# A diffusion layer on one core: key/value projection in groups of two, four and four chunks, and the modulation loads put last with three of their eight blocks kept whole

## The chip, the core and the metric

The kernel runs on one core of a Trainium2 chip. A core has a matrix engine (TensorE, PE in the views), three engines for elementwise work (VectorE or DVE, ScalarE or ACT, GpSimd or POOL), a queue engine that issues transfers (SyncE, SP) and sixteen DMA engines behind it. Each engine runs its own instructions in order and waits on semaphores for the others. The metric is the device time of one execution in microseconds; the median of several runs counts.

## What is computed

One layer of a diffusion backbone. Everything the change touches lies at its start: the modulation vectors, the modulated norm of the tokens, and the keys and values.

```python
def adaln(cvec, w_mod, b_mod):
    m = jax.nn.silu(cvec) @ w_mod + b_mod          # (1024) @ (1024, 6144)
    return jnp.split(m, 6, axis=-1)                # shift 1, scale 1, gate 1, shift 2, ...

def modulate(x, g, shift, scale):
    return rmsnorm(x, g) * (1 + scale) + shift

def keys_values(h, w_kv, k_gain):
    k, v = jnp.split(h @ w_kv, 2, axis=-1)         # (n, 1024) @ (1024, 256)
    k = rmsnorm(k.reshape(b, n, N_KV_HEADS, HEAD_DIM), k_gain)
    return k, v.reshape(b, n, N_KV_HEADS, HEAD_DIM)

def hybrid_layer(...):
    sh1, sc1, ... = adaln(c, w_mod, b_mod)         # for the 1024 latent tokens
    csh1, csc1, ... = adaln(c_ctx, w_mod, b_mod)   # for the 256 context tokens
    hl, hc = modulate(xl, g_mix, sh1, sc1), modulate(xc, g_mix, csh1, csc1)
    kc, vc = keys_values(hc, w_kv, k_gain)
    kl, vl = keys_values(hl, w_kv, k_gain)
    ...   # queries, attention, spatial gating, output projection, mixture of 16 experts
```

All is in float32, and the weights of the experts make up most of the bytes that are read.

## The kernel before

A product that has to be as good as float32 is made of three products of a rounded format, float32r: each operand is split into a rounded part `hi` (ScalarE casts, line 147) and the rest `lo` (a subtraction, line 148, on VectorE or GpSimd), and TensorE adds hi·hi, hi·lo and lo·hi. `split_to` does this for weights.

**Modulation.** Of the 6144 columns of `w_mod` the start needs 2048, shift and scale. They come as eight blocks of 512 rows by 512 columns (1 MB each, `mod_load`), two blocks to a group of 512 columns. `mod_rows` splits a block and multiplies it by `c4`, which holds the two conditioning vectors, hi and lo, as four columns: the vectors are the stationary side, the 512 weight columns stream past, 4 row slices times 2 products a block (lines 255 and 256), and the result is four rows of 512 numbers in `pr`. `mod_columns` copies these rows out (line 260) and turns them into columns with four small float32 products against `sel4` (line 262; each is two instructions in the trace). All land in `pm1`; `modc` adds the bias (line 296) and `G1` is the gain times one plus the scale (line 297).

**Tokens.** There are ten chunks of 128 tokens, 0 to 7 latent and 8 and 9 context. `x_load` loads one (0.5 MB), `x_prep` squares and sums it on ScalarE (line 165), takes the root on VectorE and GpSimd (lines 84 and 85) and scales the chunk on VectorE (line 168). `x_steps` is a generator that lets the first half of the next chunk run ahead of the second half of this one. `modulate` works on one slice j of 128 channels of one group of chunks: TensorE turns each chunk's slice (line 187), ScalarE multiplies by `G1` and adds the shift into `h` (line 191, two buffers), VectorE rounds (line 193), and VectorE or GpSimd subtracts (line 195; `LOW_P` names the slices whose subtraction goes to GpSimd).

**Keys and values.** `kv_group` takes one group of chunks, runs over the eight slices, and per slice and chunk issues three products of 256 columns (lines 219 to 221), with `modulate` two slices ahead and one or two steps of a `side` generator behind each slice. Groups are chunks 0 to 3, 4 to 7, and 8 and 9. During the first group the side work is `x_steps` of chunks 4 to 7; during the other two it is that of 8 and 9 and then `w_steps`, which splits eight quarter blocks of the next projection with GpSimd subtracting.

The order of all this is written out by hand, instruction by instruction (`manual_schedule`); no scheduler moves anything. SyncE's queue is: blocks 0 and 1, small vectors, blocks 2 to 7, chunks 0 to 3, the key/value weights, chunks 4 to 7, the next weights (2 MB), chunks 8 and 9. Behind the stage the projections of the gating and the queries start (lines 722 to 724).

Further down `g_unit` makes other columns of the modulation with float32 products that stay whole, four for each of eight groups (line 397):

```python
            for b_ in range(4):
                nc.tensor.matmul(gs["pm"][:, b_:b_ + 1], gs[cb - 1][:, b_ * P:(b_ + 1) * P], onec, start=True, stop=True)
```

Of the kernel before, what the change touches and what calls it, by code (L numbers as in the profile page):

```python
# [47 lines left out]
def layer(ctx: ExitStack, tc: tile.TileContext, a, out, dbg=None):  # L48
# [62 lines left out]
    def gm_tiles(dt):  # L111
        return [gms.tile([P, 2048], dt, name=f"gm{i}") for i in range(2)]
# [67 lines left out]
    LOW_P = ((2, 4, 6), (), ())  # L180

    def modulate(g, n, j):

        i = 1 if g == 2 else 0
        pt = psA.tile([P, 512], F32, name="tp", bufs=3)[:, :n * P]
        for t in range(n):
            nc.tensor.transpose(pt[:, t * P:(t + 1) * P], XS[g * 4 + t][:, j * P:(j + 1) * P], ident)
        h = xs.tile([P, 512], F32, name="h", bufs=2)[:, :n * P]
        pv, hv = (w.rearrange("p (t c) -> p t c", t=n) for w in (pt, h))
        parts = [(slice(0, 2), HA[0]), (slice(2, 4), HA[1])] if g == 0 else [(slice(0, n), HH1 if g == 1 else HHC[0])]  # L190
        nc.scalar.activation(h, pt, AF.Identity, scale=G1[:, j, i:i + 1], bias=B1[:, j, i:i + 1])
        for t, hi in parts:
            nc.vector.tensor_copy(hi[:, :, j, :], hv[:, t])
        for t, hi in parts:
            (nc.gpsimd if j in LOW_P[g] else nc.vector).tensor_tensor(HL[g][:, t, j, :], hv[:, t], hi[:, :, j, :].bitcast(F32),
                                                                      op=OP.subtract)

    def kv_group(g, side, steps):

        n = 2 if g == 2 else 4  # L200
        ps = [psA.tile([P, 512], F32, name="pj", bufs=4) for _ in range(n)]
        if g == 0:
            modulate(g, n, 0)
            modulate(g, n, 1)
            split_to(*wkv2, rkv[:, 2:4, :])
        for j in range(DJ):
            if j + 2 < DJ:
                modulate(g, n, j + 2)
            elif g < 2:

                if g == 1 and j + 2 == DJ:
                    gmc = [w.rearrange("p (t j c) -> p t j c", t=2, j=DJ) for w in gm_tiles(F32R)]
                    HHC.append(gmc[0])
                    HL.append(gmc[1])
                modulate(g + 1, 4 if g == 0 else 2, j + 2 - DJ)
            for t in range(n):
                hh = (HHC[0][:, t] if g == 2 else h_part(0, g * 4 + t))[:, j, :]
                hl = HL[g][:, t, j, :]
                nc.tensor.matmul(ps[t][:, :256], hh, wkv[j // 4][0][:, j % 4, :], start=(j == 0), stop=False)
                nc.tensor.matmul(ps[t][:, :256], hh, wkv[j // 4][1][:, j % 4, :], start=False, stop=False)  # L220
                nc.tensor.matmul(ps[t][:, :256], hl, wkv[j // 4][0][:, j % 4, :], start=False, stop=(j == DJ - 1))
            for _ in range(steps[j]):
                next(side, None)
        for t in range(n):
            kt = g * 4 + t
            nc.scalar.copy(kraw[:, kt], ps[t][:, :128].rearrange("p (g d) -> p g d", g=NKV))
            nc.scalar.copy(V[:, kt * NKV:(kt + 1) * NKV], ps[t][:, 128:256].rearrange("p (g d) -> p g d", g=NKV))
# [7 lines left out]
    wraw += [rawp.tile([P, 4, 512], F32, name="raw") for _ in range(2)]  # L235
    CB = (2, 3, 0, 1)

    def mod_load(n):
        nc.sync.dma_start(wraw[n], rows(a["w_mod"], n % 2 * 512, 512, CB[n // 2] * 512, 512))

    def mod_rows(n):
        jh = n % 2
        if jh == 0:
            XS["pr"] = psA.tile([P, 512], F32, name="pj", bufs=4)
        pr = XS["pr"]
        pair = w_pair()
        if n < 7:
            for h in range(2):
                split_to(*pair[h], wraw[n][:, h * 2:h * 2 + 2, :])
        for jj in range(4):  # L250
            j = jh * 4 + jj
            wh, wl = w_part(pair, jj)
            if n == 7:
                split_to(wh, wl, wraw[n][:, jj, :])
            nc.tensor.matmul(pr[:4, :], c4[:, j, :], wh, start=(j == 0), stop=False)
            nc.tensor.matmul(pr[:4, :], c4[:, j, :], wl, start=False, stop=(j == DJ - 1))

    def mod_columns(n, pr):
# [13 lines left out]
    pr = None  # L272
    for n in range(8):
        mod_rows(n)
        if n == 2:
            pv = psA.tile([P, 512], F32, name="tp", bufs=3)
            nc.tensor.transpose(pv[:, :NV], vecs, ident[:NV, :NV])
            nc.vector.tensor_copy(colv, pv[:, :NV])
            gmixc, gffnc, bmodc, bsc, gfc = (colv[:, i:j] for i, j in ((16, 24), (24, 32), (32, 80), (80, 88), (88, 96)))
        if n % 2 == 0 and n:  # L280
            mod_columns(n // 2 - 1, pr)
        pr = XS["pr"]
        if n == 3:
            rkv = wraw[2]
            for h in range(2):
                nc.sync.dma_start(rkv[:, h * 2:h * 2 + 2, :].rearrange("p a b -> p (a b)").rearrange(
                    "p (j c) -> p j c", j=4), rows(a["w_in"], h * 512, 512, 512, 256))
            for kt in range(4, 8):
                x_load(kt)
    wkv = w_pair()  # L290
    xst = x_steps(range(4))
    next(xst)
    mod_columns(3, pr)
    for _ in range(2):
        next(xst)
# [1385 lines left out]
```

## Time and profile before

| | |
|---|---|
| median of 3 runs | 1770.59 us (1770.58 to 1771.48) |
| the profiled execution | 1771.12 us, of which the span of its instructions is 1769.4 us |
| TensorE busy | 1704.0 us (96%) |
| VectorE busy | 1558.7 us (88%) |
| ScalarE busy | 1269.7 us (72%) |
| GpSimd busy | 510.0 us (29%) |
| mean granted TensorE clock | 0.987 of 2.4 GHz |
| first key/value product | 38.21 us |
| first product behind the stage | 80.67 us |

Times in the views count from the first instruction. A row of a timeline gives the start, the length, the engine, the source line, what is written from what, how many were merged, and in brackets how long the engine had been idle and what released it. Products overlap in the array, so the length of one (0.40 us at 512 columns) is more than the distance to the next (0.23 us). A row of stretches gives, for each engine, busy time and number of instructions, then the granted TensorE clock (1.00 is 2.4 GHz, 0.50 is 1.2 GHz), the DMA engines' share and GB/s.

### The profile page before, as it was taken

How to read it: one execution, taken by the hardware profiler on the slowest of the kernel's cores; microseconds unless marked ns; L12 is line 12 of the kernel's file. 1: busy time of each engine (PE TensorE's matmuls, PEld its weight loads, DVE VectorE, ACT ScalarE, POOL GpSimd, SP SyncE). 2: the span in 40 equal slices, each digit the busy share in tenths (PEclk: the TensorE clock that was granted, in tenths of full speed). 3: DMA queues.
4: the chain of work that ended last, by engine and by line, in shares of the span. 5: the costliest groups of instructions: out<-in, count | busy, mean ns of one | idle time of the engine just before them, and what ended most of it. 6: DMA issues, size and time to landing. Idle time of an engine off the chain costs nothing.

```text
span 1769.4 us, 24698 instructions
## 1 busy us (share of the span) xinstructions
PE 1704.0 (96%) x8586; PEld 1406.0 (79%) x8586; DVE 1558.7 (88%) x2329; ACT 1269.7 (72%) x1705; POOL 510.0 (29%) x358
## 2 busy tenths in 40 slices
PE   7999989999999979999999999999999999999997
PEld 3888878888888758777778888888888888888885
DVE  7778777888748999999999999999999999999997
ACT  6632367888853357777778887887878878878886
POOL 1433466788831203232330110101101101101013
PEclk9999999999999979999999999999999999999999
DMA  9357200000035678999999999999999999999994
GB/s 356 99 158 235 84 1 1 25 25 1 13 136 211 214 288 307 363 361 362 341 373 383 392 382 383 386 385 374 389 383 377 387 384 377 389 386 385 374 329 182
DMA packets 204973, 485.71 MB, mean 275 GB/s; under 512 B 10448, under 2 KB 12848, under 8 KB 204848
## 3 DMA queue, kind: packets, MB, share of 16 engines
q1 hardware_dynamic: 200096, 466.83, 71.3%
q0 software_dynamic: 4752, 17.30, 3.8%
q8 instruction: 67, 1.10, 0.3%
q14 instruction: 58, 0.48, 0.1%
HBM read 463.13 MB, written 20.97 MB: 274 GB/s over the span
## 4 chain that ended last, share of the span: by engine, by line
PE 83%; DVE 11%; issue 3%; ACT 2%; POOL 1%; DMA 0%; POOLq 0%; SPq 0%; DVEq 0%; ACTq 0%
PE p L1598 25%; PE p L1601 12%; PE py L1588 6%; PE py L1587 6%; PE py L1589 6%; PE po L801 4%; DVE wlo L148 2%; PE pj L722 2%; PE pj L724 2%; PE pj L723 2%; PE tp L1387 2%; PE st L779 2%; PE st L778 2%; PE ap L661 1%; PE pj L1023 1%
## 5 line engine op out<-in xcount | busy, mean ns | idle before, releaser
L148 DVE TENSOR_TENSOR wlo<-raw,whi 128x1024 fp32r<-128x1024 f32 (+1 forms) x544 | 646.4, 1231 | 43.2 <-ACT whi L147 39.4
L147 ACT CAST whi<-raw 128x1024 fp32r<-128x1024 f32 (+1 forms) x578 | 585.6, 1029 | 114.2 <-PE p L1601 67.8
L789 POOL TENSOR_TENSOR pl<-pf,ph 128x512 fp32r<-128x512 f32 x160 | 207.8, 1322 | 52.6 <-ACT ph L787 32.9
L1598 PE MATMUL p<-whi,xb 128*128 128x512 f32 x512 | 205.0, 400 | 0.0
L1598 PE MATMUL p<-whi,xa 128*128 128x512 f32 x512 | 204.7, 400 | 0.0
L1598 PE MATMUL p<-wlo,xa 128*128 128x512 f32 x512 | 200.0, 391 | 0.3 <-DVE wlo L148 0.2
L1598 PE MATMUL p<-wlo,xb 128*128 128x512 f32 x512 | 199.8, 390 | 0.0
L1588 PE MATMUL py<-wlo,thl 128*128 128x512 f32 x504 | 198.4, 394 | 0.0
L1587 PE MATMUL py<-whi,thl 128*128 128x512 f32 x504 | 197.6, 392 | 0.0
L1589 PE MATMUL py<-whi,thl 128*128 128x512 f32 x504 | 196.3, 389 | 0.0
L1601 PE MATMUL p<-whi,xb 128*128 128x512 f32 x512 | 158.1, 390 | 0.4 <-DVE xb L1550 0.4
L1601 PE MATMUL p<-whi,xa 128*128 128x512 f32 x512 | 158.0, 390 | 0.0
L148 DVE TENSOR_TENSOR wlo<-H,whi 128x1024 fp32r<-128x1024 f32 x106 | 131.6, 1266 | 9.6 <-ACT whi L147 8.6
L148 DVE TENSOR_TENSOR wlo<-gm,whi 128x1024 fp32r<-128x1024 f32 (+1 forms) x111 | 133.1, 1220 | 6.5 <-ACT whi L147 6.0
L147 ACT CAST whi<-H 128x1024 fp32r<-128x1024 f32 x110 | 115.9, 1054 | 24.2 <-PE p L1601 17.9
L147 ACT CAST whi<-gm 128x1024 fp32r<-128x1024 f32 (+1 forms) x111 | 114.7, 1045 | 15.7 <-PE py L1589 8.3
L1405 POOL DMA_INDIRECT acc<-ye,idx x15 | 38.1, 2539 | 292.1 <-DVE ye L1402 292.1
L787 ACT CAST ph<-pf 128x512 fp32r<-128x512 f32 x160 | 99.3, 621 | 28.4 <-PE po L801 25.8
L1601 PEld LDWEIGHTS p<-whi,xb 128*128 128x128 f32 x512 | 96.0, 188 | 21.7 <-DVE xb L1550 0.8
L1601 PEld LDWEIGHTS p<-whi,xa 128*128 128x128 f32 x512 | 96.1, 188 | 20.9
L1598 PEld LDWEIGHTS p<-wlo,xa 128*128 128x128 f32 x512 | 96.3, 188 | 19.5 <-DVE wlo L148 1.1
L1587 PEld LDWEIGHTS py<-whi,thl 128*128 128x128 f32 x504 | 94.6, 188 | 21.6
(379 smaller groups left out, 3691.4 us busy)
## 6 DMA issues: line engine op xcount, KB each, us to landing
raw<-in_w_dram SPq DMA_DIRECT2D x271, 1024.0 KB, 8.3
H<-in_w_dram SPq DMA_DIRECT2D x55, 1024.0 KB, 8.0
gm<-in_w_dram SPq DMA_DIRECT2D x54, 1024.0 KB, 8.5
raw<-in_w_mod_dram SPq DMA_DIRECT2D x64, 256.0 KB, 3.2
raw<-in_w_mod_dram SPq DMA_DIRECT2D x4, 1024.0 KB, 7.5
raw<-in_w_in_dram SPq DMA_DIRECT2D x16, 256.0 KB, 4.0
raw<-in_w_out_dram SPq DMA_DIRECT2D x4, 1024.0 KB, 5.1
xr<-in_x_dram SPq DMA_DIRECT2D x8, 512.0 KB, 6.2
```

The source lines that it names most:

```text
L147: nc.scalar.copy(hi, src)
L148: (eng or nc.vector).tensor_tensor(lo, src, hi.bitcast(F32), op=OP.subtract)
L722: nc.tensor.matmul(p, hh[:, j, :], hi, start=(j == 0), stop=False)
L787: nc.scalar.copy(ph, pf)
L789: nc.gpsimd.tensor_tensor(pl, pf, ph.bitcast(F32), op=OP.subtract)
L801: nc.tensor.matmul(U["po", u][:, sl], st[:, blk], mv[:, sl], start=(k == 0 and o == 0 and n == 0), stop=(k == NK - 1 and n == 2), skip_gro ...
L1405: nc.gpsimd.indirect_dma_start(out=acc, out_offset=bass.IndirectOffsetOnAxis(ap=idx[:, e:e + 1], axis=0), in_=G["ye"], in_offset=None, com ...
L1587: nc.tensor.matmul(PY[e][cb], th, hi[:, sl], start=fst, stop=False)
L1588: nc.tensor.matmul(PY[e][cb], th, lo[:, sl], start=False, stop=False)
L1589: nc.tensor.matmul(PY[e][cb], tl, hi[:, sl], start=False, stop=lst)
L1598: nc.tensor.matmul(p, xh[:, j, :], w[:, jj, :], start=(j == 0 and w is pr[0]), stop=False)
L1601: nc.tensor.matmul(p, xl[:, j, :], pr[0][:, jj, :], start=False, stop=(j == DJ - 1))
```

## The change

Three things are changed at the start of the kernel; from the gating projection on, each engine's instructions stand in the order of before.

1. **Groups.** `GROUPS` makes the first key/value group of chunks 0 and 1, the second of 2 to 5 and the third of 6 to 9, so that the context chunks are in the last group, beside two latent ones. In that group ScalarE's shift is two instructions of 256 columns a slice, since latent and context have different vectors. GpSimd also subtracts slices 2, 4 and 6 of the second group. The rounded context slices live in a ring of four slots in one buffer.
2. **Queue.** The loads are: blocks 0 to 3, chunk 0, block 4, chunk 1, block 5, the key/value weights, blocks 6 and 7 as four quarters each, chunks 2 to 7. The key/value weights are split, and the first three slices of chunks 0 and 1 turned, before blocks 6 and 7 are used.
3. **Whole blocks.** Blocks 3, 5 and 7 (`FULL`) are not split. `mod_full` multiplies them as float32: 16 products a block, in which the 128 by 128 weights are the stationary side and two columns of `csil` (the two conditioning vectors) stream past; the sums add to `pm1` directly.

```diff
+    GROUPS = ((0,), (1, 2), (3, 4))
+    LOW_P = ((2, 4, 6), (2, 4, 6), ())
...
+    def turn(g, j):
+
+        pt = XS["pt", g, j] = psA.tile([P, 512], F32, name="tp", bufs=3)
+        for i, kt in enumerate(2 * q + t for q in GROUPS[g] for t in range(2)):
+            nc.tensor.transpose(pt[:, i * P:(i + 1) * P], XS[kt][:, j * P:(j + 1) * P], ident)
+
+    def modulate(g, j):
+
+        if ("pt", g, j) not in XS:
+            turn(g, j)
+        n = len(GROUPS[g]) * 2 * P
+        pt = XS.pop(("pt", g, j))
+        h = xs.tile([P, 512], F32, name="h", bufs=2)
+        for i, sl in ((0, slice(0, 2 * P)), (1, slice(2 * P, n))) if g == 2 else ((0, slice(0, n)),):
+            nc.scalar.activation(h[:, sl], pt[:, sl], AF.Identity, scale=G1[:, j, i:i + 1], bias=B1[:, j, i:i + 1])
+        hv = h.rearrange("p (q t c) -> p q t c", q=2, t=2)
+        for k, q in enumerate(GROUPS[g]):
+            nc.vector.tensor_copy(h_pair(q, j)[0], hv[:, k])
+        for k, q in enumerate(GROUPS[g]):
+            hi, lo = h_pair(q, j)
+            (nc.gpsimd if j in LOW_P[g] else nc.vector).tensor_tensor(lo, hv[:, k], hi.bitcast(F32), op=OP.subtract)
...
-            for _ in range(steps[j]):
+            for _ in range(2 if g == 0 and j < 2 else 1):
                 next(side, None)
...
+    FULL = (3, 5, 7)
+
     def mod_load(n):
-        nc.sync.dma_start(wraw[n], rows(a["w_mod"], n % 2 * 512, 512, CB[n // 2] * 512, 512))
+        src = rows(a["w_mod"], n % 2 * 512, 512, CB[n // 2] * 512, 512)
+        if n < 6:
+            nc.sync.dma_start(wraw[n], src)
+        else:
+            for jj in range(4):
+                nc.sync.dma_start(wraw[n][:, jj, :], src[:, jj, :])
...
+    def mod_full(n, jjs):
+        for jj in jjs:
+            for b in range(4):
+                nc.tensor.matmul(pm1[:, CB[n // 2] * 4 + b, :], wraw[n][:, jj, b * P:(b + 1) * P], csil[:, 4 + jj, :],
+                                 start=False, stop=False, skip_group_check=True)
...
-    for n in range(2, 8):
-        mod_load(n)
-    for kt in range(4):
+    mod_load(2)
+    mod_load(3)
+    x_load(0)
+    mod_load(4)
+    x_load(1)
+    mod_load(5)
+    mod_rows(0)
+    mod_rows(1)
+    pv = psA.tile([P, 512], F32, name="tp", bufs=3)
+    nc.tensor.transpose(pv[:, :NV], vecs, ident[:NV, :NV])
+    nc.vector.tensor_copy(colv, pv[:, :NV])
...
+    mod_rows(2)
...
+    mod_load(6)
+    mod_load(7)
+    for kt in range(2, 8):
         x_load(kt)
...
+    mod_columns(0)
+    mod_full(3, range(4))
+    mod_columns(1)
+    xst = x_steps((0, 1))
+    next(xst)
+    mod_rows(4)
+    next(xst)
+    mod_full(5, range(4))
+    mod_columns(2)
+    for _ in xst:
+        pass
     wkv = w_pair()
...
+    for h in range(2):
+        split_to(*wkv[h], rkv[:, h * 2:h * 2 + 2, :])
+    for j in range(3):
+        turn(0, j)
+    mod_rows(6)
+    mod_full(7, range(4))
+    mod_columns(3)
...
-    kv_group(0, x_steps(range(4, 8)), (1, 1, 2, 2, 2, 1, 1, 1))
-    ws = chain(x_steps((8, 9)), w_steps())
-    kv_group(1, ws, (1,) * 8)
-    kv_group(2, ws, (1,) * 8)
+    ws = chain(x_steps(range(2, 6)), x_steps(range(6, 10)), w_steps())
+    for g in range(3):
+        kv_group(g, ws)
```

TensorE, from the end of block 2 to the end of block 4 (`pj` are the sums of rows, `pk` is `pm1`, `HL1` and `HH1` hold raw blocks 3 and 5). Before, block 3 follows as eight wide products and the columns of blocks 0 and 1 were made in the middle of block 2:

```order
L256 MATMUL pj_191<-wlo_195,c4_80 4x512
L277 MATMUL tp_208<-ident_68,vecs_119 128x96
L262 MATMUL pk_130<-sel4_71,h_211 128x2 x4
L255 MATMUL pj_191<-whi_217,c4_80 4x512
L256 MATMUL pj_191<-wlo_218,c4_80 4x512
```

And now:

```order
L276 MATMUL pj_188<-wlo_192,c4_80 4x512
L289 MATMUL pk_130<-sel4_71,h_223 128x2 x4
L281 MATMUL pk_130<-csil_79,HL1_133 128x2 x16
L289 MATMUL pk_130<-sel4_71,h_245 128x2 x4
L275 MATMUL pj_261<-whi_262,c4_80 4x512
L276 MATMUL pj_261<-wlo_263,c4_80 4x512
```

Between the wide products of blocks 2 and 4 there now stand 24 narrow ones in a row, of two columns each, where eight wide ones and four narrow ones stood.

ScalarE, around the start of the key/value stage (`jk,r` are the squares, `gm` holds chunks 4 to 7). Before, the squares of the first four chunks stand ahead of the first shift:

```order
L147 CAST whi<-raw 128x512 x4
L165 ACTIVATE jk,r<-x 128x1024 x4
L147 CAST whi<-HL_133 128x1024
L191 ACTIVATE h<-tp,modc,G_83 128x512 x2
L147 CAST whi<-HL_133 128x1024
L191 ACTIVATE h<-tp,modc,G_83 128x512
```

And now:

```order
L147 CAST whi<-raw 128x512 x4
L207 ACTIVATE h<-tp,modc,G_83 128x256 x3
L165 ACTIVATE jk,r<-x 128x1024 x2
L207 ACTIVATE h<-tp,modc,G_83 128x256
L165 ACTIVATE jk,r<-gm_128 128x1024
```

The squares of chunks 2 to 5 now stand behind the first three shifts, so behind `G1`, and among the shifts of the first group.

SyncE's queue. Before:

```order
L239 DMA HL1_133<-in_w_mod_dram 128x4x512 x2
L239 DMA HH1_134<-in_w_mod_dram 128x4x512 x2
L239 DMA raw_135<-in_w_mod_dram 128x4x512
L239 DMA raw_136<-in_w_mod_dram 128x4x512
L157 DMA x_150<-in_x_dram 128x1024
```

And now:

```order
L157 DMA x_146<-in_x_dram 128x1024
L256 DMA HH1_134<-in_w_mod_dram 128x4x512
L157 DMA x_149<-in_x_dram 128x1024
L256 DMA HH1_134<-in_w_mod_dram 128x4x512
L311 DMA HL1_133<-in_w_in_dram 128x4x256 x2
L259 DMA raw_135<-in_w_mod_dram 128x512 x4
L259 DMA raw_136<-in_w_mod_dram 128x512 x4
```

Two chunks and the key/value weights, 2 MB together, have moved ahead of the last two blocks.

## Rows read from the trace of the kernel before

**Rows 1.** The page of the whole run: the chain that ended last, shares by engine.

```profile
PE 83%; DVE 11%; issue 3%; ACT 2%; POOL 1%; DMA 0%; POOLq 0%; SPq 0%; DVEq 0%; ACTq 0%
```

**Rows 2.** Stretches: busy us of each engine, granted clock, DMA share, GB/s.

```profile
80.60:130.00 49.40, 49.40 (x256) 42.05 (x256) 32.29 (x53) 18.78 (x39) 15.87 (x13) 1.00 0.59 190
```

**Rows 3.** Timeline of ScalarE: start, length, line, operation, then idle time and its releaser.

```profile
23.52 2.00 ACT L147 CAST whi<-raw 128x1024 fp32r<-128x1024 f32 x2 [0.71 <-DMA raw<-in_w_mod_dram]
...
26.23 2.18 ACT L147 CAST whi<-raw 128x512 fp32r<-128x512 f32 x4 [0.71 <-DMA raw<-in_w_mod_dram]
```

**Rows 4.** Timeline of VectorE and TensorE around the third modulation block.

```profile
13.68 2.36 DVE L148 TENSOR_TENSOR wlo<-HL,whi 128x1024 fp32r<-128x1024 f32 x2 [0.71 <-ACT whi L147]
...
14.53 0.40 PE L255 MATMUL pj<-whi,c 128*4 128x512 f32 x1
...
17.13 0.26 DVE L278 COPY colv<-tp 128x96 f32<-128x96 f32 x1 [1.10 <-PE tp L277]
```

**Rows 5.** Timeline of TensorE at 2.4 GHz, and one line's group over the run.

```profile
28.49 1.05 PE L262 MATMUL pk<-sel,h 4*128 4x2 f32 x8
...
29.47 0.39 PE L255 MATMUL pj<-whi,c 128*4 128x512 f32 x1
...
29.70 0.40 PE L256 MATMUL pj<-wlo,c 128*4 128x512 f32 x1
...
102.48 0.95 PE L397 MATMUL pk<-onec,g 128*128 128x1 f32 x8
...
L397 PE MATMUL pk<-onec,g x64: 164/250/250, 102.5 to 200.3; 128*128 128x1 f32 x64
```

**Rows 6.** Timeline of TensorE later in the run, at 1.2 GHz, two wide products.

```profile
240.62 0.63 PE L778 MATMUL st<-HL,K 128*128 128x512 f32 x1
...
241.04 0.63 PE L779 MATMUL st<-HL 128*128 128x512 f32 x1
```

**Rows 7.** TensorE later in the run: sixteen narrow products, and the stretch they fill.

```profile
269.18 2.28 PE L764 MATMUL tp<-wr,modl 128*128 128x16 f32 x16
...
270.00:271.00 1.00, 1.00 (x9) 1.00 (x8) 0.00 (x0) 0.04 (x1) 0.00 (x0) 0.71 0.00 0
```

**Rows 8.** Timeline from the end of the modulation to the first key/value product.

```profile
33.34 0.19 DVE L296 TENSOR_TENSOR modc<-pk,colv 128x32 f32<-128x32 f32 x1 [0.42 <-PE pk L262]
...
33.57 0.17 DVE L297 SCALAR_TENSOR_TENSOR G<-modc,colv 128x16 f32<-128x16 f32 x1
...
35.57 0.75 DVE L168 TENSOR_SCALAR x<-x,r 128x1024 f32<-128x1024 f32 x1 [0.44 <-POOL r L85]
...
36.38 2.18 PE L187 MATMUL tp<-ident,x 128*128 128x128 f32 x9 [0.72 <-DVE x L168]
...
38.21 0.56 PE L219 MATMUL pj<-whi,H 128*128 128x256 f32 x1
```

**Rows 9.** Stretches around the start of the key/value stage: the granted clock.

```profile
35.00:41.00 6.00, 5.10 (x23) 4.81 (x24) 5.31 (x13) 4.07 (x7) 0.53 (x1) 0.50 1.03 397
...
42.00:48.00 6.00, 6.00 (x54) 6.00 (x53) 4.70 (x14) 5.08 (x10) 4.32 (x7) 1.00 0.34 123
```

**Rows 10.** Stretches of the second and the third key/value group as they run before.

```profile
54.77:69.30 14.53, 14.53 (x125) 14.38 (x123) 11.18 (x19) 10.63 (x23) 6.48 (x6) 1.00 0.04 12
...
69.30:80.67 11.37, 8.32 (x60) 7.21 (x59) 9.94 (x15) 6.38 (x17) 6.33 (x5) 1.00 0.04 11
```

**Rows 11.** Groups by form, 0 to 82 us: ScalarE's shifts and squares.

```profile
L191 ACT ACTIVATE h<-tp,modc,G 128x256 f32<-128x256 f32 x8 | 4.5, 566 | 4.8 <-DVE gm L195 3.3 <-DVE HL L195 0.7 <-PE tp L187 0.4
...
L165 ACT ACTIVATE jk<-x 128x1024 bf16<-128x1024 f32 x6 | 6.4, 1070 | 1.2 <-issue 1.1
```

**Rows 12.** VectorE's rounding alone and beside GpSimd, and GpSimd's subtractions, same stretch.

```profile
70.51 0.28 DVE L193 CAST gm<-h 128x256 fp32r<-128x256 f32 x1
...
72.28 1.08 DVE L193 CAST gm<-h 128x256 fp32r<-128x256 f32 x1 [0.22 <-ACT h L191]
...
L148 POOL TENSOR_TENSOR wlo<-raw,whi 128x512 fp32r<-128x512 f32 x8 | 11.4, 1438 | 6.5 <-ACT whi L147 6.1
```

More of the change, by code (lines that the diff above doesn't have):

```diff
@@ L178, in x_steps @@
             yield
[L180 to L196, printed above, removed]
@@ L198, in kv_group, with h_pair @@
-    def kv_group(g, side, steps):
-        n = 2 if g == 2 else 4
-        ps = [psA.tile([P, 512], F32, name="pj", bufs=4) for _ in range(n)]
+    GROUPS = ((0,), (1, 2), (3, 4))
+    LOW_P = ((2, 4, 6), (2, 4, 6), ())
+    def h_pair(q, j):
+        if q == 4:
+            return XS["ctx"][:, j % 4, 0], XS["ctx"][:, j % 4, 1]
+        if q < 2:
+            return HA[q][:, :, j, :], HL[0][:, q * 2:q * 2 + 2, j, :]
+        return HH1[:, q * 2 - 4:q * 2 - 2, j, :], HL[1][:, q * 2 - 4:q * 2 - 2, j, :]
@@ L202, in kv_group @@
+    def kv_group(g, side):
+        kts = [2 * q + t for q in GROUPS[g] for t in range(2)]
+        ps = [psA.tile([P, 512], F32, name="pj", bufs=4) for _ in kts]
         if g == 0:
-            modulate(g, n, 0)
-            modulate(g, n, 1)
-            split_to(*wkv2, rkv[:, 2:4, :])
+            modulate(g, 0)
+            modulate(g, 1)
         for j in range(DJ):
             if j + 2 < DJ:
-                modulate(g, n, j + 2)
+                modulate(g, j + 2)
             elif g < 2:
@@ L211, in kv_group @@
                 if g == 1 and j + 2 == DJ:
[L212 to L221, printed above, removed]
@@ L222, in kv_group @@
-            for _ in range(steps[j]):
+                    XS["ctx"] = gms.tile([P, 2048], F32R, name="gm0").rearrange("p (s w t c) -> p s w t c", s=4, w=2, t=2)
+                modulate(g + 1, j + 2 - DJ)
+            for i, kt in enumerate(kts):
+                hh, hl = (w[:, kt % 2, :] for w in h_pair(kt // 2, j))
+                nc.tensor.matmul(ps[i][:, :256], hh, wkv[j // 4][0][:, j % 4, :], start=(j == 0), stop=False)
+                nc.tensor.matmul(ps[i][:, :256], hh, wkv[j // 4][1][:, j % 4, :], start=False, stop=False)
+                nc.tensor.matmul(ps[i][:, :256], hl, wkv[j // 4][0][:, j % 4, :], start=False, stop=(j == DJ - 1))
@@ L223, in kv_group @@
+            for _ in range(2 if g == 0 and j < 2 else 1):
                 next(side, None)
[L224 to L227, printed above, removed]
+        for i, kt in enumerate(kts):
+            nc.scalar.copy(kraw[:, kt], ps[i][:, :128].rearrange("p (g d) -> p g d", g=NKV))
+            nc.scalar.copy(V[:, kt * NKV:(kt + 1) * NKV], ps[i][:, 128:256].rearrange("p (g d) -> p g d", g=NKV))
@@ L267, in layer @@
         nc.sync.dma_start(vecs[r0:r0 + nr], a[src].rearrange("(r p) -> r p", p=P))
-    for n in range(2, 8):
-        mod_load(n)
-    for kt in range(4):
-        x_load(kt)
[L272 to L289, printed above, removed]
-    wkv = w_pair()
[L291 to L295, printed above, removed]
+    mod_load(2)
[9 more added lines that the diff above has]
+    nc.vector.tensor_copy(colv, pv[:, :NV])
+    gmixc, gffnc, bmodc, bsc, gfc = (colv[:, i:j] for i, j in ((16, 24), (24, 32), (32, 80), (80, 88), (88, 96)))
+    mod_rows(2)
+    rkv = wraw[2]
+    for h in range(2):
+        nc.sync.dma_start(rkv[:, h * 2:h * 2 + 2, :].rearrange("p a b -> p (a b)").rearrange("p (j c) -> p j c", j=4),
+                          rows(a["w_in"], h * 512, 512, 512, 256))
+    mod_load(6)
+    mod_load(7)
+    for kt in range(2, 8):
+        x_load(kt)
+    mod_columns(0)
[9 more added lines that the diff above has]
+        pass
+    wkv = w_pair()
+    for h in range(2):
+        split_to(*wkv[h], rkv[:, h * 2:h * 2 + 2, :])
[4 more added lines that the diff above has]
+    mod_columns(3)
     nc.vector.tensor_tensor(modc, pm1, bmodc[:, :16].unsqueeze(2).to_broadcast([P, 16, 2]), op=OP.add)
@@ L298, in layer @@
                                    op0=OP.add, op1=OP.mult)
-    for _ in xst:
-        pass
-    split_to(*wkv[0], rkv[:, 0:2, :])
     c0 = 768 + 512
@@ L313, in w_steps @@
                 yield
-    wkv2 = wkv[1]
     wkv = [[w.rearrange("p a b -> p (a b)").rearrange("p (j c) -> p j c", j=4) for w in h] for h in wkv]
```

23 lines of the change are left out of this document (11 added, 12 removed).

## The prediction

> **What bounds the kernel now.** I read the chain that ended last first: TensorE is 83% of it [rows 1]. Then the table of stretches: right behind the key/value stage TensorE is busy for all of 49.4 us [rows 2], and its instructions from there on are those of before. So what the change is worth is the time at which the stage ends, 80.67 us [rows 10]; later work moves with it one to one. Then the timelines of the first 81 us, where three things set the pace in turn. To 26 us it is the transfers: ScalarE waits for one modulation block after the other, and they land 2.71 us apart (23.52 to 26.23, both released by the DMA) [rows 3]. From 33.74 us, when `G1` is done, it is chunk 3, whose root and scaling hold TensorE until 36.38, and the first key/value product starts at 38.21 [rows 8]. Then it is TensorE: the stage takes 80.67 − 38.21 = 42.46 us, the second group 14.53 of it with TensorE busy throughout, the third 11.37 with TensorE busy for 8.32 [rows 10]. At the stage's start the granted clock is 1.2 GHz (0.50 from 35 to 41 us), because TensorE had little to do before; it is back at 2.4 by 42 us, after some 3.5 us of dense products [rows 8, 9].
>
> **Queue and early chunks.** The change takes chunk 3's chain out of the way: chunks 0 and 1 are scaled before the last blocks come. That could give 38.21 − 33.74 = 4.5 us, less the shift, rounding and first wait that remain, about 1.0 (one shift of 0.57 and one rounding of 0.28 [rows 11, 12], and two semaphores): 3.5 us. Against it, 2 MB more must land before the last block: block 7 now lands at about 26.2 + 2 × 2.71 = 31.6 us. With the block's last eight instructions (0.9), `mod_columns` (1.0), `modc` and `G1` (0.4) and that 1.0 the first product would start at 34.9, and 3.3 of the 3.5 us would stay. But the transfers don't set the pace, as the next part shows.
>
> **Whole blocks.** Each of the blocks 3, 5 and 7 trades two casts, two subtractions and eight wide products for 16 float32 products with 128 by 128 stationary weights. The nearest rows are line 397's, of the same weights with one column: its 32 products are 64 instructions, two each, and eight of them take 0.95 us, (0.95 − 0.25)/7 = 0.10 apart [rows 5]. Line 262's stand (1.05 − 0.25)/7 = 0.114 apart [rows 5]. So a block is 32 instructions at 0.11, **3.5 us**, where eight wide products 0.23 apart (29.47 to 29.70) took 1.9 [rows 5]. The Trainium skill, "FP8 and Floating Point Precision", section "TensorE Precision Notes", says that true float32 takes four passes through the array; by it a block would cost 7 us at 2.4 GHz and the three together 10.5 us more than I count, but line 397's 64 instructions for 32 products show two here.
>
> The splits that go were beside other work, so they give nothing at the end; TensorE's list becomes the path. Block 2's subtractions take 2.36 us on VectorE, from 13.68 before [rows 4]; now the copy of `colv` (0.26, behind a turn that waits for block 1's last product at 14.5) stands ahead of them, so they start at about 15.1 and end at 17.5. With the copy of the sums behind them, `mod_columns(0)` starts at 18.2. From there TensorE's row is: four times `mod_columns` at 0.98 (28.49 to 29.47) [rows 5], 3.9; three whole blocks, 10.6; 16 wide products of blocks 4 and 6 at 0.23, 3.7; six turns at 0.11, 0.7. That is 18.9 us, to **37.1 us**, 3.6 us behind what the transfers alone would ask (31.6 + 0.9 + 1.0 = 33.5). With 0.4 for `modc` and `G1` [rows 8] and the 1.0 from above the first product starts at 38.5: at 2.4 GHz the early chunks' gain is eaten, +0.3.
>
> **The clock.** The narrow instructions in a row are what I doubt most. At 269.18 us the trace has a run of 16 products of 16 columns; TensorE is busy without a gap from 270 to 271, and the granted clock falls in that very microsecond (0.71 is its mean) [rows 7]. Being busy with narrow products did not hold 2.4 GHz there. Between the wide products of blocks 2 and 4 now stand 48 narrow instructions (32, and 8 on either side), some 5.4 us, and 40 each behind those of blocks 4 and 6. The Trainium skill, "TensorE: Matmul & The Clock Gate", section "Why this matters for your kernels", asks only that TensorE have no idle gaps between bursts; by that wording the clock would stay, which is the second rival below. At 1.2 GHz wide products are 0.42 apart [rows 6], and turns (36.38 to 38.21 − 36.38 = 1.83 for nine) 0.20 [rows 8, 9]; narrow ones load the same 128 columns of weights, so I take 0.21. If the clock falls at about 22 us and stays down, the remaining 15.1 us of TensorE's list cost 1.9 times as much: +13.6 us. The eight wide products of a split block last 8 × 0.42 = 3.4 us at 1.2 GHz, as long as it took the key/value products to bring 2.4 back, so it may come back in between, and fall again. Between +0 and +13.6 I take two thirds, **+9 us**: the fall has a row of its own, the return rests on a burst that is only just as long.
>
> **The key/value stage.** Group one now needs eight shifts (0.47 apart; 0.57 each [rows 11]) and four squares of chunks 2 to 5 (1.07 and the read of the sum, 1.2 [rows 11]) from ScalarE behind `G1`. Up to chunk 5's square that is 5 × 0.47 + 4 × 1.2 = 7.1 us, then root, scaling (0.75 [rows 8]), four turns, a shift and the rounding, 3.4: group two starts 10.5 us behind `G1`, 9.5 behind the first product. TensorE's own work in it is 48 products at 0.12 and 18 turns, 7.7 us, so it waits for ScalarE. GpSimd's subtractions of slices 2, 4 and 6, slower than VectorE's, can make it 12 (an estimate: some 0.5 to 0.8 us each); I take 10.5. Group two has the work of the old second group, 14.5 [rows 10]. Group three has 96 products and 24 turns, 14.1; but VectorE and GpSimd hinder each other: a rounding of 0.28 takes 1.08 beside GpSimd, whose eight subtractions average 1.44 [rows 12]. Their sum there, eight times 1.25 on VectorE (an estimate: two roundings and two somewhat longer subtractions a slice) and 11.5 on GpSimd, is 21.5 us in a stretch of 17.8: between 0 and 3.7 us of waits, I take 2.5, as the old third group had 3.05 (11.37 − 8.32) in the same fix. Together 41.6 instead of 42.46: **−0.9** (−3.4 to +1.8). If the stage begins at 1.2 GHz, group one's products take 0.21 instead of 0.12 for a while: +1.5 (0 to 3.5).
>
> **Sum.** +0.3 + 9 − 0.9 + 1.5 = +9.9 us on the profiled execution's 1771.12, whose span of 1769.4 has 1.7 us around it; that execution is 0.5 above the median of the runs, so I forecast 1770.59 + 9.9 = **1780.5 us**. About 0.2%, 3.5 us, can be told from no change.
>
> **Rivals.**
> - *The narrow products slow the clock* (the forecast), 0.67. It spans +5 (one fall, a quick return) to +17 (down from 22 us into the stage, 13.6 + 3.5).
> - *The clock holds at 2.4 GHz*, 0.21. For it: in the mod stage of before the clock held through four runs of eight narrow instructions. Then +0.3 − 0.9 is −0.6, within −3.5 and +3: **1770.0 us**, no change.
> - *The narrow products pass as fast as the blocks land*, 0.12, and the kernel is faster. Its place is the three whole blocks; it decides if 32 instructions take under 2.7 us, 0.085 apart, at 2.4 GHz. Line 397's 0.10 is not far from that, and two columns need hardly any streaming. Then the transfers set the pace: the first product starts at 34.9, −3.3, and with the stage at its likely −0.9: −4.2, **1766.4 us**; with the best of the stage, −3.4, it is 1763.9. Against it: the two nearest rows are both above 0.085, and block 2's late split moves the start.
> - That the change doesn't do what it says can't be: the orders show it.
>
> **How the numbers follow.** The range reaches from the second case's lower part to the first's upper end: 1769 to 1788; it leaves out the third case and some of the tails, two in ten. Slower by over 0.2%: the first case nearly whole and a little of the second, 0.69. Within 0.2%: most of the second and a third of the third, 0.22. Faster: the rest of the third, 0.09.
>
> **What will show it.** Right, if the granted clock is 0.50 in a stretch between 20 and 45 us, the whole blocks' instructions stand 0.21 apart there, and the first key/value product starts at 44 to 52 us. If the clock is 1.00 and the blocks take 3.5 us, the first product starts at 38 to 39 us. The stage's length should be 41 to 45 us, with TensorE waiting for ScalarE's shifts in group one and for VectorE in group three. I am wrong in the main if narrow products turn out under 0.085 apart, if the clock holds, or if work behind the stage does not move with it.

## The result and the profile after

The changed kernel takes **1782.86 us** (median of 4 runs, 1782.36 to 1783.01) beside 1770.82 us for the kernel before in the same comparison: 1.0065 times as long, 95% interval 1.0052 to 1.0078, or 12.0 us more. The forecast was 1780.5 us, 9.9 more. In the profiled execution the span is 1781.2 us instead of 1769.4, +11.8, and the mean granted clock is 0.983 instead of 0.987.

The page of the changed kernel, busy time and chain by engine, in place of [rows 1]:

```profile
PE 1714.8 (96%) x8658; PEld 1420.6 (80%) x8658; DVE 1551.2 (87%) x2336; ACT 1265.1 (71%) x1707; POOL 509.4 (29%) x361
...
PE 82%; DVE 10%; issue 3%; ACT 1%; POOL 1%; POOLq 0%; DVEq 0%; ACTq 0%
```

TensorE is still nearly the whole chain; it has 72 more instructions and 10.8 us more busy time than before (1704.0). Stretches there (columns as in [rows 2]; the clock is the third number from the end):

```profile
18.00:22.00 4.00, 4.00 (x28) 3.64 (x26) 0.97 (x4) 1.34 (x3) 0.57 (x1) 0.82 1.04 394
22.00:26.00 4.00, 4.00 (x20) 3.98 (x20) 3.02 (x3) 2.73 (x3) 0.55 (x1) 0.50 1.08 357
26.00:30.00 4.00, 4.00 (x13) 1.87 (x14) 0.00 (x0) 3.25 (x5) 0.00 (x0) 0.50 1.05 387
30.00:34.00 4.00, 4.00 (x34) 3.91 (x32) 3.42 (x4) 0.00 (x0) 0.00 (x0) 0.90 1.04 405
34.00:38.00 4.00, 4.00 (x18) 3.34 (x18) 2.60 (x5) 0.00 (x0) 0.00 (x0) 0.52 1.03 410
```

TensorE is busy for 4.00 of every 4 us, and still the clock is 0.50 from 22 to 30 us and again around 36; of these 20 us VectorE is busy for 10.0 and ScalarE for 7.3. From there the clock comes back once more and falls once more. Its timeline shows why that costs so much (before, the eight instructions of line 262, the same as those of line 289 now, took 1.05 us [rows 5]):

```profile
18.34 1.05 PE L289 MATMUL pk<-sel,h 4*128 4x2 f32 x8
19.32 5.92 PE L281 MATMUL pk<-csil,HL 128*128 128x2 f32 x32
25.17 1.86 PE L289 MATMUL pk<-sel,h 4*128 4x2 f32 x8
30.34 3.84 PE L281 MATMUL pk<-csil,HH 128*128 128x2 f32 x32
34.11 1.82 PE L289 MATMUL pk<-sel,h 4*128 4x2 f32 x8
...
40.61 3.82 PE L281 MATMUL pk<-csil,raw 128*128 128x2 f32 x32
44.36 1.84 PE L289 MATMUL pk<-sel,h 4*128 4x2 f32 x8
...
47.68 0.58 PE L232 MATMUL pj<-whi,H 128*128 128x256 f32 x1 [1.48 <-DVE H L210]
```

The three whole blocks take 5.9, 3.8 and 3.8 us, the one with the fall in it longest, and between them everything runs at half speed: the columns take 1.8 us instead of 1.05. The first key/value product comes at 47.68 us instead of 38.21 [rows 8], **+9.5 us**. ScalarE has by then stood idle for 17 us:

```profile
46.74 1.02 ACT L207 ACTIVATE h<-tp,modc,G 128x256 f32<-128x256 f32 x2 [17.09 <-DVE G L337]
```

The rest of the loss is in the key/value stage. The first products of group two (for two of its chunks, then for the other two), of group three and of the next projection, and at 74.25 us a turn of group three's first slice that waits:

```profile
60.44 0.37 PE L232 MATMUL pj<-whi,H 128*128 128x256 f32 x1
...
62.51 0.39 PE L232 MATMUL pj<-whi,HH 128*128 128x256 f32 x1 [1.12 <-ACT V L239]
...
74.25 0.33 PE L197 MATMUL tp<-ident,x 128*128 128x128 f32 x1 [1.06 <-DVE x L168]
...
78.46 0.39 PE L232 MATMUL pj<-whi,HH 128*128 128x256 f32 x1
...
94.33 0.40 PE L756 MATMUL pj<-whi,H 128*128 128x512 f32 x1
```

The groups take 12.76, 18.02 and 15.87 us, together 46.65 where the stage took 42.46 [rows 10]: **+4.2 us**. So the next projection starts 94.33 − 80.67 = 13.66 us later, and 11.8 of these reach the end of the span.

### The profile page after: what moved, and what is told of

It is laid out like the page before. It is cut to its first block, busy times and chain, and to the rows that moved or that the text cites. A ratio compares the mean times of both kernels' runs of the same rounds, so it can differ in the third digit from the quotient of the medians.

```text
span 1781.2 us, 24870 instructions
## 1 busy us (share of the span) xinstructions
PE 1714.8 (96%) x8658; PEld 1420.6 (80%) x8658; DVE 1551.2 (87%) x2336; ACT 1265.1 (71%) x1707; POOL 509.4 (29%) x361
## 4 chain that ended last, share of the span: by engine, by line
PE 82%; DVE 10%; issue 3%; ACT 1%; POOL 1%; POOLq 0%; DVEq 0%; ACTq 0%
PE p L1632 24%; PE p L1635 12%; PE py L1622 6%; PE py L1621 6%; PE py L1623 6%; PE po L835 4%; DVE wlo L148 2%; PE pj L756 2%; PE pj L758 2%; PE pj L757 2%; PE st L813 2%; PE tp L1421 2%; PE st L812 2%; PE pj L1057 2%; PE pj L1059 1%
```

## The experiments

Each kernel's two marks, from its timeline of TensorE; "stage" is the distance between them. Ratios are against the kernel before, timed in the same session (its median was 1771.09 us beside e1 to e4, 1771.25 beside e5 to e8 and 1771.73 beside e9 to e11). The marks are those of one execution each: in before, e9 and e10, which are the same up to the first product, it comes at 38.21 to 38.73 us; in the changed kernel and e6, also the same up to there, at 47.68 and 47.63.

| kernel | first key/value product | next projection | stage | median us | ratio, 95% interval |
|---|---|---|---|---|---|
| before | 38.21 | 80.67 | 42.46 | 1770.82 | |
| changed | 47.68 | 94.33 | 46.65 | 1782.86 | 1.0065 (1.0052 to 1.0078) |
| e1_all_split | 41.93 | 88.58 | 46.65 | 1777.24 | 1.0033 (1.0020 to 1.0045) |
| e2_whole_alone | 53.35 | 96.22 | 42.87 | 1786.19 | 1.0089 (1.0072 to 1.0105) |
| e3_wide_zero | 39.12 | 85.76 | 46.64 | 1775.06 | 1.0022 (1.0012 to 1.0031) |
| e4_groups_alone | 39.38 | 87.11 | 47.73 | 1775.81 | 1.0024 (1.0014 to 1.0034) |
| e5_early_squares | 47.48 | 91.10 | 43.62 | 1781.00 | 1.0063 (1.0045 to 1.0081) |
| e6_split_on_vector | 47.63 | 92.17 | 44.54 | 1781.55 | 1.0058 (1.0040 to 1.0076) |
| e7_wide_zero_early | 40.53 | 84.50 | 43.97 | 1773.59 | 1.0015 (1.0005 to 1.0025) |
| e8_last_block_whole | 41.70 | 83.62 | 41.92 | 1773.37 | 1.0013 (1.0003 to 1.0023) |
| e9_before_vector | 38.46 | 77.82 | 39.36 | 1768.99 | 0.9981 (0.9972 to 0.9990) |
| e10_before_shared | 38.73 | 79.62 | 40.89 | 1768.92 | 0.9983 (0.9974 to 0.9992) |
| e11_wide_early_vector | 41.00 | 82.82 | 41.82 | 1771.88 | 1.0005 (0.9996 to 1.0014) |

### Which part costs it: e1, e2 and e4

**e1_all_split** takes the whole blocks out of the change.

```diff
-    FULL = (3, 5, 7)
+    FULL = ()
...
-    mod_full(3, range(4))
+    mod_rows(3)
```

and so for blocks 5 and 7.

> The changed kernel with blocks 3, 5 and 7 split and multiplied wide, as the other five are; the new queue, the early chunks and the groups of two, four and four stay. Theory (the products with two moving columns take the clock away and cost 0.11 us each): TensorE's clock stays at 1.00 from 14 us on, the first key/value product comes at 34 to 38 us in place of 47.7, and the kernel takes 1770 to 1774 us. Rival (the new queue or the order of the chunks delays the start, whatever the products are): first product at 44 us or later, 1779 us or more.

It is 5.6 us faster than the changed kernel (the intervals of the two ratios do not overlap), with 6.2 us above before left. The stage is 46.65 us to the hundredth, so its length has nothing to do with the blocks. But the first product comes at 41.93, not at 34 to 38, so both theories of e1 were wrong in size. With eight splits in this order VectorE is busy throughout, TensorE for 2.55 of 4 us, and behind that pause it runs at half clock again; two stretches of e1:

```profile
30.00:34.00 4.00, 2.55 (x18) 1.61 (x18) 4.00 (x6) 2.33 (x4) 0.00 (x0) 0.98 1.04 408
34.00:38.00 4.00, 4.00 (x12) 1.17 (x12) 3.55 (x6) 0.00 (x0) 0.00 (x0) 0.59 1.02 406
```

**e2_whole_alone** puts nothing but the whole blocks into the kernel before.

```diff
...
-        mod_rows(n)
+        if n in FULL:
+            mod_full(n, range(4))
+        else:
+            mod_rows(n)
```

> The kernel before with one part of the change alone: blocks 3, 5 and 7 unsplit in float32; queue, chunks and groups of before. Theory: the clock falls to 0.50 within some us of the first narrow products and the first key/value product moves from 38.2 to 46 to 50 us; the key/value stage stays at 42.5 us; 1778 to 1783 us. Rival (narrow products cost only their 0.11 us at the full clock, the clock falls for another reason of the new order): first product at 38 to 41 us, 1771 to 1774 us.

It is the slowest of all, +15 us, above the expected 1778 to 1783, and its first product is later than the expected 46 to 50; the stage hardly moves (42.87). One stretch and the first product:

```profile
22.00:38.00 16.00, 16.00 (x66) 12.83 (x67) 3.44 (x6) 5.44 (x8) 1.12 (x2) 0.50 1.05 394
```

```profile
53.35 0.56 PE L219 MATMUL pj<-whi,H 128*128 128x256 f32 x1
```

The clock is 0.50 for 16 us in a row, without a pause of TensorE, although the eight wide products of block 4 (25.16 to 28.7 us) lie in that stretch. The whole blocks alone cost 15.1 us at the first product; beside the new queue and the early chunks it is 9.5. The difference, 5.7 us, is what queue and chunks give together with the clock, which comes back twice before the first product in the changed kernel and once in e2 (1.00 from 41 to 43 us); the two parts were not taken apart.

**e4_groups_alone** keeps modulation and queue of before and takes the new groups, with the second half of the key/value weights split ahead of them.

```diff
...
-    split_to(*wkv[0], rkv[:, 0:2, :])
+    for h in range(2):
+        split_to(*wkv[h], rkv[:, h * 2:h * 2 + 2, :])
...
+    GROUPS = ((0,), (1, 2), (3, 4))
...
+    ws = chain(x_steps(range(4, 10)), w_steps())
```

> The kernel before with the groups of two, four and four chunks and the new share of GpSimd's subtractions; modulation and queue of before, and the second half of the key/value weights split ahead of the stage. If the groups are worth what was forecast, the stage takes 41 to 42 us in place of 42.5 and the kernel 1769 to 1771 us. Theory from the trace of the changed kernel: the stage takes 44 to 46 us also from a start at the full clock, and the kernel takes 1772 to 1775 us. Rival (the longer stage there came from its start at half clock): 42 us and 1770 us.

+4.7 us, and the stage takes 47.73, more than either theory had: the groups, with GpSimd's new share in them, are a loss by themselves. TensorE waits for VectorE's roundings twice, for 3.62 us ahead of the first product, so outside the stage, and for 2.50 us inside it. The rival is not settled by e4, whose stage starts at 0.50 too (39.38 to 43.38 us) and has 0.57 once more from 54 to 58 us, behind the second wait. But the kernel before starts its stage at half clock for just as long as the changed one; the first 4 us of the two stages, before and then changed:

```profile
38.21:42.21 4.00, 4.00 (x22) 4.00 (x21) 3.33 (x10) 3.92 (x6) 0.85 (x2) 0.56 1.04 387
```

```profile
47.68:51.68 4.00, 4.00 (x20) 4.00 (x21) 2.12 (x7) 3.49 (x8) 1.61 (x3) 0.55 0.31 121
```

So the start at half clock is not what makes the stage longer than before.

### What pulls the clock down: e3

```diff
+    WW = 64
+    csw = QD.rearrange("p a b c -> p (a b c)")[:, :4 * WW].rearrange("p (j w) -> p j w", j=4)
+    nc.gpsimd.memset(csw, 0.0)
...
+    nc.vector.tensor_copy(csw[:, :, 0:2], csil[:, 4:8, :])
...
-                nc.tensor.matmul(pm1[:, CB[n // 2] * 4 + b, :], wraw[n][:, jj, b * P:(b + 1) * P], csil[:, 4 + jj, :],
+                k = 2 * (CB[n // 2] * 4 + b)
+                nc.tensor.matmul(pk1[:, k:k + WW], wraw[n][:, jj, b * P:(b + 1) * P], csw[:, jj, :],
```

> The changed kernel with 64 moving columns in each product of the three whole blocks in place of 2: the 62 columns beside the two of the modulation are zeros and add nothing. Number of instructions and weight loads is unchanged. Theory (the clock falls because few columns move under the weight loads): the clock stays at 1.00 or falls for less long, the products stay 0.11 to 0.13 us apart, first key/value product at 38 to 42 us, 1773 to 1778 us. Rival (the weight loads or the float32 passes pull the clock down): the clock at 0.50 for as long as in the changed kernel, first product at 47 to 50 us, 1782 to 1786 us. Second rival (the 64 columns are paid for in full): spacing of 0.2 us or more at the full clock, first product at 46 us or later.

The same number of instructions and of weight loads, with 62 columns of zeros more in each, is **7.8 us faster** than the changed kernel. The stretch from 18 to 38 us, and TensorE's timeline:

```profile
18.00:38.00 20.00, 19.49 (x150) 16.57 (x149) 10.82 (x17) 7.34 (x10) 1.13 (x2) 1.00 1.05 390
```

```profile
18.78 3.79 PE L287 MATMUL pk<-qd,HL 128*128 128x64 f32 x32
...
25.81 3.68 PE L287 MATMUL pk<-qd,HH 128*128 128x64 f32 x32
...
32.98 3.68 PE L287 MATMUL pk<-qd,raw 128*128 128x64 f32 x32
...
39.12 0.39 PE L236 MATMUL pj<-whi,H 128*128 128x256 f32 x1 [1.48 <-DVE H L214]
```

The clock is 1.00 for all 20 us, the 64 columns pass in the time of two (32 instructions in 3.7 us, 0.11 apart), and the first product is at 39.12. The weight loads and the number of instructions are those of the changed kernel, so they alone did not lower it; what differs between the two kernels is the columns that move under each. The difference, 47.68 − 39.12 = **8.6 us**, is the clock's share. The stage is the same again (46.64).

### Why the stage is longer: e5 and e6

**e5_early_squares** moves the squares and scalings of chunks 2 to 5 ahead of the stage.

```diff
     mod_rows(6)
+    xst = x_steps(range(2, 6))
+    for _ in xst:
+        pass
     mod_full(7, range(4))
...
-    ws = chain(x_steps(range(2, 6)), x_steps(range(6, 10)), w_steps())
+    ws = chain(iter((None,) * 8), x_steps(range(6, 10)), w_steps())
```

> The changed kernel with the squares and scalings of chunks 2 to 5 done ahead of the key/value stage, while TensorE works on the last blocks, in place of inside the first group. Theory (ScalarE paces group one: four squares lie among its eight modulations, and the scaled chunks come late to the next group's transposes): the first key/value product stays at 47 to 48 us, the waits for the scaled chunks (1.5 and 1.1 us) go, and the stretch from the first key/value product to the first product of the next projection falls from 46.6 to 43 to 44.5 us; 1779.5 to 1781.5 us. Rival (the stage is paced by VectorE beside GpSimd in the last two groups): stretch at 46 us or more, 1782.5 to 1784 us.

First products of the three groups and of the next projection:

```profile
47.48 0.58 PE L232 MATMUL pj<-whi,H 128*128 128x256 f32 x1 [1.48 <-DVE H L210]
...
57.21 0.37 PE L232 MATMUL pj<-whi,H 128*128 128x256 f32 x1
...
75.24 0.39 PE L232 MATMUL pj<-whi,HH 128*128 128x256 f32 x1
...
91.10 0.40 PE L759 MATMUL pj<-whi,H 128*128 128x512 f32 x1
```

Group one takes 9.73 us instead of 12.76, and these 3.0 us are all that the stage gains; groups two and three (18.03 and 15.86) are as they were. Group one as a stretch, in the changed kernel and then in e5:

```profile
47.68:60.44 12.76, 10.77 (x71) 9.92 (x71) 8.66 (x25) 9.33 (x19) 5.23 (x7) 0.86 0.40 123
```

```profile
47.48:57.21 9.73, 9.73 (x71) 9.73 (x71) 5.31 (x17) 5.41 (x11) 2.21 (x3) 0.82 0.34 111
```

TensorE is busy throughout in e5, for 10.77 of 12.76 us in the changed kernel, at much the same clock. There it had stood before a turn of group two's first slice, with group one's last two slices behind it (the row of the changed kernel):

```profile
58.05 0.33 PE L197 MATMUL tp<-ident,gm 128*128 128x128 f32 x1 [1.51 <-DVE gm L168]
```

Of the two waits that were to go, this one is gone and the 1.1 us for the scaling of a later chunk stayed. The 3.0 us are read from the trace; the ratios of e5 and of the changed kernel overlap too much to show them in the time.

**e6_split_on_vector** moves eight subtractions of the next projection's weights from GpSimd to VectorE.

```diff
-                split_to(*w_part(wb[jh], jj), wraw[jh][:, jj, :], nc.gpsimd)
+                split_to(*w_part(wb[jh], jj), wraw[jh][:, jj, :])
```

> The changed kernel with the eight subtractions of the next projection's weight split, which GpSimd does during the last two groups, on VectorE. Theory (VectorE's casts take 1.3 us in place of 0.28 and its subtractions 1.5 in place of 0.41 while GpSimd runs): these come down to 0.3 to 0.4 us, VectorE has eight subtractions of about 0.8 us more, the stretch from the first key/value product to the next projection falls from 46.6 to 44 to 46 us; 1780 to 1782.5 us. Rival (VectorE is full in the last group either way): 46.5 to 48 us, 1783 to 1785 us.

VectorE's groups by form in group three (busy, mean ns of one), of the changed kernel and then of e6:

```profile
L213 DVE TENSOR_TENSOR gm<-h,gm 128x256 fp32r<-128x256 f32 x7 | 6.2, 888 | 0.0
L210 DVE CAST gm<-h 128x256 fp32r<-128x256 f32 x6 | 3.9, 651 | 0.1
L210 DVE CAST HH<-h 128x256 fp32r<-128x256 f32 x6 | 3.7, 620 | 0.0
```

```profile
L148 DVE TENSOR_TENSOR wlo<-raw,whi 128x512 fp32r<-128x512 f32 x7 | 4.8, 685 | 0.0
L213 DVE TENSOR_TENSOR gm<-h,gm 128x256 fp32r<-128x256 f32 x7 | 2.9, 419 | 0.0
...
L210 DVE CAST gm<-h 128x256 fp32r<-128x256 f32 x6 | 1.8, 292 | 0.4 <-ACT h L207 0.2
L210 DVE CAST HH<-h 128x256 fp32r<-128x256 f32 x6 | 1.7, 288 | 0.7 <-ACT h L207 0.7
```

With GpSimd silent a rounding takes 0.29 us instead of 0.65 and a subtraction 0.42 instead of 0.89; VectorE does 4.8 us of extra work and is still less busy (11.23 of 13.77 us beside 14.70 of 15.87). The Trainium skill, "SBUF — State Buffer", section "SBUF: two separate sides", calls the port pair that the two engines share an exclusive lock, not a split of bandwidth. The trace agrees: in the changed kernel's group three every instruction of VectorE takes either 0.28 to 0.42 us or 1.29 to 1.54, and none lies between. Group three then has TensorE busy almost throughout (stretch of e6):

```profile
78.40:92.17 13.77, 13.74 (x116) 13.74 (x117) 11.23 (x32) 10.85 (x29) 0.00 (x0) 1.00 0.22 62
```

13.77 us instead of 15.87: 2.1 us were the two engines in each other's way. This too is read from the trace, since the ratios of e6 and of the changed kernel overlap; e9 below shows it in the time.

### Do the repairs add up: e7, e8, e11, and the kernel before with one of them: e9, e10

**e7** is e3 with two squares and one scaling early; **e11** is e7 with e6's edit; **e8** is e11 with `FULL = (7,)`.

```diff
+    xst = x_steps(range(2, 6))
+    next(xst)
     mod_columns(3)
+    next(xst)
...
+    ws = chain(xst, iter((None,) * 2), x_steps(range(6, 10)), w_steps())
```

> The kernel with 64 moving columns (e3_wide_zero) and, beside it, two squares and one scaling of the later chunks ahead of the key/value stage. Theory of ScalarE's pace in group one: first product at 39.0 to 39.5 us, the stretch to the next projection 44 to 45.5 us in place of 46.6, 1772.5 to 1774.5 us. Rival: no change of the stretch, 1775 us; or the squares wait for their chunks and hold up the modulation, first product at 40 us or later, 1776 us or more.

> e7_wide_zero_early with only the last block whole (blocks 3 and 5 split and wide, two instructions 0.22 us apart for what takes eight narrow ones), and the next projection's subtractions on VectorE. If TensorE's list paces the start at the full clock: blocks 3 and 5 are 1.7 us shorter each, first product at 37 to 38.5 us, 1769 to 1773 us, at or below the kernel before. If the two more splits on ScalarE and VectorE, or idle TensorE and with it the clock, decide: first product at 39.5 to 42 us, 1773 to 1778 us.

> The changed kernel with 64 moving columns, two squares and a scaling early (e7_wide_zero_early), and the next projection's subtractions on VectorE. If the three repairs add up: first product at 39 to 40.6 us, stretch to the next projection 41 to 42.5 us, 1770 to 1772.5 us, level with the kernel before. If not: 1773 us or more.

The stage does what was expected: 43.97, and 41.92 and 41.82 with both repairs, 0.5 to 0.6 below before. The first product does not. In e7 and e11 it slips to 40.5 and 41.0, though nothing was put on TensorE: the clock falls once after all. The wait ahead of it is 1.48 us as in e3, so the early squares do not hold it up. A stretch of e7:

```profile
30.00:34.00 4.00, 4.00 (x16) 2.25 (x16) 1.86 (x4) 0.00 (x0) 0.00 (x0) 0.57 1.04 409
```

So with 64 columns the clock stayed up in e3's execution and not in those of e7 and e11, whose instructions on TensorE are the same up to the fall. In e8, where VectorE subtracts for seven blocks, TensorE waits for it inside the last of these (1.45 us, 32.07 to 33.52), the clock falls too (0.60 from 24 to 28 us), and the start comes at 41.70. The repaired change, e11, is level with the kernel before by its median: 1.0005. But three of its eleven runs took 1775.9 to 1777.1 us, at a mean clock of 0.984 to 0.985, and the other eight 1770.5 to 1773.0, at 0.987 to 0.989.

**e9_before_vector** is e6's edit on the kernel before; **e10_before_shared** leaves every other subtraction on GpSimd.

> The kernel before with one edit: the eight subtractions of the next projection's weight split, on GpSimd during the last two groups, on VectorE. The 2.7 us for which TensorE waits for VectorE's subtractions in the last group of before lie beside GpSimd's. Theory (VectorE is slowed fourfold beside GpSimd): the waits shrink to under 1 us, first key/value product unchanged at 38.2 us, the stretch to the next projection 39.5 to 41.5 us in place of 42.5, 1768 to 1770 us. Rival (eight subtractions of 0.68 us fill VectorE as much): 42 to 43.5 us, 1770.5 to 1772 us.

> As e9_before_vector, with every other one of the eight subtractions on VectorE and four left on GpSimd. Theory: between the two, 40 to 42 us, 1769 to 1770.5 us; below e9_before_vector only if VectorE's work paces the last group rather than its slowness beside GpSimd.

Next projection and VectorE's forms in the last group of e9, whose rows of before are [rows 12]:

```profile
77.82 0.40 PE L722 MATMUL pj<-whi,H 128*128 128x512 f32 x1
```

```profile
L148 DVE TENSOR_TENSOR wlo<-raw,whi 128x512 fp32r<-128x512 f32 x5 | 3.4, 684 | 0.0
L195 DVE TENSOR_TENSOR gm<-h,gm 128x256 fp32r<-128x256 f32 x7 | 3.0, 425 | 0.2
L193 DVE CAST gm<-h 128x256 fp32r<-128x256 f32 x6 | 1.7, 288 | 1.0 <-ACT h L191 1.0
```

The stage falls from 42.46 to 39.36 us, and the kernel is 0.19% faster than before (interval 0.10 to 0.28%), the fastest of the study with e10. By the trace e10 keeps half of the contention (stage 40.89); by the time the two can't be told apart.

## Why the prediction was right, and what was off

**The clock**, the doubtful term, held. Forecast: a fall at about 22 us, products 0.21 apart, +9 us from the clock within 0 to 13.6. Measured: the fall at some 20.5 us, inside the first whole block; line 289's eight in 1.84 us, each about 0.35 long, so 0.21 apart; and 8.6 us by e3. The second and third block passed at the full clock, though, 32 instructions in 3.8 us. The guess that a split block's wide products bring 2.4 GHz back, and that it falls again, is what the changed kernel shows twice. It is not certain in each execution: in e6, whose modulation is the same, the first whole block passed at the full clock, block 4's wide products did not bring it back, and the second whole block took 6.8 us:

```profile
18.93 3.73 PE L281 MATMUL pk<-csil,HL 128*128 128x2 f32 x32
...
27.30 6.82 PE L281 MATMUL pk<-csil,HH 128*128 128x2 f32 x32
```

Its first product still comes at 47.63. That the two thirds of 13.6 us, which rested on no row, came out so near is partly luck: in e2, where it came back once, the whole blocks cost 15.1 us. In e2 TensorE was busy for 16.00 of 16 us at a clock of 0.50. The Trainium skill, "TensorE: Matmul & The Clock Gate", section "Why this matters for your kernels", asks that there be no idle gaps; here that was not enough. The rival built on it is out, and so is the third: at the full clock the narrow products are 0.11 to 0.12 apart (32 in 3.7 to 3.8 us), not under 0.085.

**The list at 2.4 GHz** was forecast to give a first product at 38.5; e3 has 39.12. `mod_columns(0)` was put at 18.2, and the row has 18.34. First product, both terms: 47.5 forecast, 47.68 measured.

**The stage** is the step that was mis-sized: forecast 41.6 with +1.5 for the clock, 43.1 in all; measured 46.65, outside the 41 to 45 that the prediction gave as a sign of being right. By groups:

- One was taken at 10.5, paced by ScalarE's squares, and 1.5 for the clock: 12.0. It took 12.76. e5 shows the pace: without the squares TensorE fills it, 9.73; the one long wait with them is for a scaling behind the squares (1.51 us), not for a shift. That 9.73 is 2.0 above the 7.7 us of TensorE's work that the forecast counted, at a mean clock of 0.82; an estimate from these, 9.73 × 0.82 = 8.0, puts about 1.8 of the 2.0 down to the clock.
- Two was taken at 14.5, from a stretch without any wait [rows 10], and took 18.02, **3.5 more**. This is the step that failed: a wait at each seam had been left out. Two of its four chunks wait for the banks of group one (1.12 us), whose copies stand on ScalarE behind two squares and a shift; a turn for group three waits for the scaling of a late chunk (1.06 us); both rows stand above. Its slices are 1.87 us each when nothing waits (at 65.20, 67.08, 68.95 and 70.83 its turns begin), 15.0 for eight, half a us more than before because the next group has four chunks to turn instead of two. With the two waits that is 17.2; the other 0.8 us were not taken apart, and no run takes the two waits away, so their price is read from the rows alone.
- Three was taken at 14.1 + 2.5 = 16.6 and took 15.87. The term for VectorE beside GpSimd, 2.5, measured 2.1 (e6).

**Work behind the stage** was to move one to one. Of 13.66 us, 11.8 reach the end. At a reduction in the routing of the experts, before and after, it is still 12.7:

```profile
L1275 DVE TENSOR_REDUCE vstar<-mm x1: 274/274/274, 628.5 to 628.5; 16x1 f32<-16x129 f32 x1
```

```profile
L1309 DVE TENSOR_REDUCE vstar<-mm x1: 274/274/274, 641.2 to 641.2; 16x1 f32<-16x129 f32 x1
```

So 1.0 us goes before it and 0.9 behind. Which waits take it up was not settled.

The sum: 9.9 forecast, + 3.6 (stage) + 0.6 (list) − 0.4 (clock) − 1.9 (given back) = 11.8, the difference of the spans. So the mechanism was right, but the number is better than its terms: half of what the stage lost beyond the forecast was given back behind it, and neither was foreseen.

## What to carry over

Unsplit narrow products trade elementwise work that was hidden for TensorE time that is not, and in this kernel a TensorE that was busy throughout with two-column products ran at half clock: before such an edit, look for a run of narrow products in the trace and read the granted clock there. When a stage is cut into smaller groups, follow the order on the bounding engine across the seam; an instruction of the next group that stands ahead of this group's last products makes every delay of the next a delay of this one, and each seam has its waits. And an idle GpSimd is no free place for elementwise work beside a VectorE that is waited for: eight subtractions moved from one to the other took 3.1 us off the stage in e9.

## What was not expected of the hardware

- Zeros in 62 more columns cost nothing (0.11 us an instruction at the full clock either way), and with them the granted clock was 1.00 for 20 us in e3, where with two columns it was 0.50 from 22 to 30 us. In e7 and e11 the clock fell once with them too.
- The clock is not the same in every execution of the same instructions: from 18 to 22 us, with the modulation code of before, it was 1.00 in e9 and 0.61 in e10 (stretches of the two, in this order).

```profile
18.00:22.00 4.00, 3.69 (x19) 1.81 (x20) 4.00 (x5) 2.90 (x3) 0.00 (x0) 1.00 1.05 387
```

```profile
18.00:22.00 4.00, 4.00 (x16) 1.94 (x17) 4.00 (x4) 3.22 (x4) 0.00 (x0) 0.61 1.04 387
```
